# Splitting fp32 weights in a three-block decoder: part of the low halves on GpSimd instead of ScalarE plus an accumulating DMA

## The chip, the cores and the metric

The kernel runs on one core of one Trainium2 chip. The metric is device time in microseconds (us), the median over several runs. A second source of numbers is one profiled execution, from which the page, the groups of instructions, the windows, the waits and the timeline below are read.

## What is computed

A decoder with three kinds of blocks runs over one sequence of 256 tokens with 1024 features, all in fp32. Sixteen meta tokens are put ahead of it in block 1, so that block 1 works on 272. Cut to what matters here:

```
x = first_block(...)    # latent attention, then a gated linear recurrence (lru)
x = second_block(...)   # two hybrid layers, see below
x = third_block(...)    # retention, block attention, feed-forward

def hybrid_layer(x):                       # twice
    h = rms_norm(x, norm1_g);  proj = h @ w_in
    q, k, v, iq, ik, iw, a_in, c_in, g_in = split(proj)
    y_attn = sparse_attention(q, k, v, iq, ik, iw) @ w_attn_out
    a = causal_dwconv(a_val * sigmoid(a_gate), conf_conv_w) + b    # 31 taps
    y_conf = silu(layer_norm(a)) @ w_conf_out
    y_sc = (c_b * causal_dwconv(c_c * c_x, sc_conv_w)) @ w_sc_out  # 3 taps
    x = x + (g0 * y_conf + g1 * y_attn + g2 * y_sc) @ w_o          # g = sigmoid(g_in)
    return x + feed_forward(rms_norm(x, norm2_g))
```

## The kernel before

Weights come from HBM in **units** of 128 x 1024 fp32 (512 KB; some 128 x 848 or smaller). A product keeps fp32 accuracy with three fast matmuls: weight and activation are each split into a high part (rounded to the fast format) and a low part, the exact difference. `mm3` (L202 to L207) multiplies high by high, low weight by high activation, high weight by low activation, for each of the eight 128-row pieces of a unit: 24 matmuls of 256 or 272 columns a unit.

`emit_unit` (L166) makes a unit ready: a DMA issued by SyncE brings `raw`, ScalarE copies it to `whi` (L175), and `wlo` is made in one of two ways. Normally VectorE subtracts (L181). For a marked unit, ScalarE writes the negated copy into `wlo` (L178) and a DMA issued by GpSimd adds `raw` onto it (L179). `raw`, `whi` and `wlo` have five buffers each. `unit` (L189) hands out the next unit and sees to it that the three after it are emitted (`AHEAD = 3`). It also sets the marks: a running sum grows by `dma_share` with each unit, and a unit that brings it to 1 is marked.

The share is 0 outside the hybrid layers. In each hybrid layer it is 0.3 from the start (L900: token-major groups and the gated inputs `w_a2`), 0.625 from L1088 (the short convolution `w_c2`, with attention as side job, then `w_so`), 0.5 from L1119 (the gates `w_g2`, `w_g1` and the attention output `w_ao`), and 0 again from L1135.

Around the weights, VectorE carries most of the other work. The largest part of it in a hybrid layer are the 31-tap convolution's 240 multiply-adds (L924, `ca<-apad,vec,ca`), spread over these stages by a side job and held in their program order; they have to be through before the layer norm that follows the gates. GpSimd adds the finished convolution tiles to a sum (L931, `lnst`) and multiplies and adds the gated branches (L1125 and L1133, `mg`). In the recurrence, GpSimd multiplies `ii` by `rr` (L716) and adds squares (L326).

A scheduler orders the instructions of each engine ahead of time by dependences and its own costs; each engine then takes its list in that order.

Of the kernel before, what the change touches and what calls it, by code (L numbers as in the profile page):

```python
# [9 lines left out]
F32 = mybir.dt.float32  # L10
# [7 lines left out]
T1 = 272          # meta tokens + frames  # L18
T = 256
# [6 lines left out]
# Column offsets of the packed per-feature vectors (value of feature k*128+p at [p, off+k]).  # L26
# [29 lines left out]
class _Null:  # L56
    """Stands for every object of a pass that only lists the weight units in their order."""
# [17 lines left out]
class Prog:  # L75
    AHEAD = 3       # weight units split ahead of the one in use

    def __init__(self, tc, ins, out, dbg=None, plan=None):
        self.tc, self.nc, self.I, self.out = tc, tc.nc, ins, out
        self.dbg = dbg or {}  # L80
        self.plan = plan          # None: this pass lists the units
        self.specs, self.emitted, self.used = [], {}, 0
        self.jobs = []
        self.dma_share, self.share = 0.0, 0.0   # part of the units whose lo a DMA adds up
# [54 lines left out]
    @staticmethod  # L139
    def stagger(gens, depth):  # L140
        """Runs the generators in order, up to depth of them in flight, each a step behind."""
        gens, active = list(gens), []
        while gens or active:
            for g in list(active):
                try:
                    next(g)
                except StopIteration:
                    active.remove(g)
            if gens and len(active) < depth:
                g = gens.pop(0)  # L150
                next(g)
                active.append(g)
            yield

# [11 lines left out]
    def emit_unit(self, i):  # L166
        nc = self.nc
        name, m, c0, n, by_dma = self.plan[i]
# [3 lines left out]
        for a, b in ((0, n),) if i else ((0, n // 2), (n // 2, n)):  # L172
# [3 lines left out]
            if by_dma:  # L176
                # lo = -hi + raw, the sum made by an accumulating DMA: spares the vector engine
                nc.scalar.activation(lo[:, c], raw[:, c], AF.Copy, scale=-1.0)  # L178
                nc.gpsimd.dma_start(lo[:, c], raw[:, c], accum_op=ALU.add)  # L179
            else:  # L180
                nc.vector.tensor_sub(lo[:, c], raw[:, c], hi[:, c].bitcast(F32))  # L181
# [7 lines left out]
    def unit(self, name, m, c0, n):  # L189
        i = self.used  # L190
        self.used += 1
        self.share += self.dma_share
        by_dma = self.share >= 1.0
        self.share -= by_dma
        self.specs.append((name, m, c0, n, by_dma))
# [13 lines left out]
    def part(self, o, unit, xs, k0, k1, kt, base=0):  # L209
        """Contraction tiles k0..k1 of the output o; the unit starts at contraction tile base."""  # L210
# [7 lines left out]
    def tile_fm(self, name, m, kt, xs, t):  # L218
        """Feature-major output tile m: sum over kt contraction tiles; xs(k) -> (hi, lo)."""
# [6 lines left out]
    def lead_fm(self, name, ms, xs, t, ks, between=None):  # L226
        """Tiles ms of 8 contraction tiles, the first ks of all of them ahead of the others."""
# [9 lines left out]
    def tiles_of_unit(self, name, m, nt, kt, xs, t):  # L237
        """nt output tiles of few contraction tiles, packed in one unit."""
# [10 lines left out]
    def rsq(self, m, n, name):  # L249
        """1/sqrt of the positive columns m[:, :n]: bit seed, three Newton steps."""  # L250
# [10 lines left out]
    def cols(self, accs, segs, name):  # L261
        """Sums over features of each acc, per token, tokens on partitions (one column a segment)."""
# [29 lines left out]
    def rows(self, col, segs, name):  # L292
        """Column form [token, 1] -> the same values along the free dim, on every partition;
        a generator with one step between the vector engine's part and the rest."""
# [15 lines left out]
    def norm_rows(self, accs, segs, scales, eps, name):  # L310
        """1/rms of each token, for each acc, as rows. A generator; the first step is empty."""
# [51 lines left out]
    def consts(self):  # L363
# [17 lines left out]
        # the tensor engine runs while it waits for the first data, and so comes to its full clock  # L381
# [4 lines left out]
    def late(self, ins):  # L386
        """Keeps an instruction behind those of its engine that come before it here."""
        self.tc.keep_in_program_order(ins)

    def after(self, ins, first):  # L390
        """Keeps an instruction behind an earlier one of its engine."""
# [4 lines left out]
    def more_consts(self):  # L396
# [10 lines left out]
        self.caus = cp.tile([128, 2, T], F32, name="caus")      # 1 where the key is later  # L407
# [5 lines left out]
    def decay_rate(self):  # L413
        """softplus(-lam) = max(-lam, 0) + log1p(exp(-|lam|)); log1p(e) = 2 atanh(e / (2 + e))"""
# [22 lines left out]
    def mla(self):  # L437
# [13 lines left out]
        # latents: tiles kv 0..1, q 2..4  # L451
# [9 lines left out]
        # shared rope key, twice down the partitions  # L461
# [27 lines left out]
        def gate_tile(i):  # L489
            o = self.tile_fm("w_a_in", 6 + i, 8, xs, T1)  # L490
            dve.tensor_mul(gate[:, i], o, rb)
            # 2 silu(x) = x (1 + tanh(x / 2)); the half follows with the product
# [9 lines left out]
        # keys and values  # L502
# [18 lines left out]
        # queries: units of two tiles  # L521
# [64 lines left out]
        def meta():  # L586
            """The meta queries of all heads, over the meta keys."""
# [59 lines left out]
    def residual(self, name, kt, xs, x, t, t0, gains, g2=None, lead=(2, 6), between=None):  # L647
        """x += w^T xs, tile by tile; then the scaled split of x and the sums of its squares
        for the norm that follows. gains: key of the gain columns (or an AP of columns)."""
# [18 lines left out]
    def lru(self):  # L668
# [8 lines left out]
        last = [None]  # L677

        def gates(g):
            """The decay and what it leaves to the input, from the gates of two feature tiles."""  # L680
# [6 lines left out]
        def block(g):  # L687
# [5 lines left out]
            if g % 2:  # L693
                gates(g - 1)
                gates(g)
                # sqrt(1 - a^2) = (1 + a) sqrt((1 - a) / (1 + a))
# [37 lines left out]
        # from here on, the frames only: nothing that follows looks at the meta tokens  # L734
# [25 lines left out]
    def final_norm(self):  # L760
        """The final norm of block 1 and the first norm of block 2 in one: columns of both."""
# [13 lines left out]
    def final_x(self):  # L775
        """The output of block 1, the residual stream of the blocks that follow."""
# [12 lines left out]
    def norm_full(self, src, g, name):  # L789
        """The normalised stream, split: src(k) * g(k) * row factor."""  # L790
# [10 lines left out]
    def proj_tok(self, name, g, n, dst):  # L801
        """Group g of a token-major projection of the un-normalised split."""
# [14 lines left out]
    def rope_tok(self, v3, nh, half, cs):  # L817
        """In place on v3 [128, nh, 2*half]; cs [128, 4*half] = cos|cos|-sin|sin."""
# [10 lines left out]
    def attend(self, pairs, nk, mask, scales, pv):  # L829
        """Softmax attention of nh heads over nk keys for one tile of 128 queries, in steps.  # L830
        pairs: (queries^T, keys^T) per head; mask [128, nk] is added; scales: a positive column
        per head; pv(pt): takes the transposed probabilities, [keys, nk/128, nh * 128]."""
# [37 lines left out]
    def hybrid(self, layer):  # L870
# [7 lines left out]
        # ---- token-major columns, first group; the normalised stream meanwhile  # L878
# [21 lines left out]
        self.dma_share = 0.3  # L900
# [8 lines left out]
        # ---- gated depthwise convolution branch: inputs; its taps are spread over what follows  # L909
# [23 lines left out]
        # ---- attention, as side jobs. Columns: index queries 512, index key 64, weights 8,  # L933
        # values 256, keys 256, queries 1024
        qT = self.big("qT", 8, T)
        kiT = self.big("kiT", 7, T)      # 0-1 keys, 2-5 index queries, 6 index key twice
# [6 lines left out]
        # gain of the query dims that are not rotated, 1 for those that are  # L943
# [58 lines left out]
        def index(j, b, hds):  # L1002
            """Index scores of the heads hds (of one parity) added up for query tile j."""
# [84 lines left out]
        self.dma_share = 0.625  # L1088
# [3 lines left out]
        # ---- short gated convolution branch  # L1092
# [17 lines left out]
        # ---- gates and outputs of the branches  # L1110
# [8 lines left out]
        self.dma_share = 0.5  # L1119
# [15 lines left out]
        self.dma_share = 0.0  # L1135
# [53 lines left out]
        # ---- feed-forward with a short convolution  # L1189
# [24 lines left out]
    def ffn(self, name, g, finish):  # L1214
        """22 pairs of feature tiles of the normed stream; finish(first, second, i) takes each.
        The first pairs use the un-normalised split, while the normalised one is made."""
# [30 lines left out]
    def third(self):  # L1247
# [4 lines left out]
        rot = rm[:, 0:512]               # cos|cos|-sin|sin, 64 each, for each token tile  # L1252
# [6 lines left out]
        # columns: rq 512, rk 512, mq 512, mk 512 | mv 512 | rv 1024  # L1259
# [60 lines left out]
        # block attention: one block of 256 keys, so plain causal attention within it  # L1320
# [3 lines left out]
        def moba(j, q4, par):  # L1324
            """Heads 4*q4 + par and 4*q4 + par + 2, whose rows start at 64 * par."""
# [21 lines left out]
        # retention: scores with keys on partitions, outputs token-major, then transposed  # L1347
# [70 lines left out]
        # retention gate, then gates, outputs, mixture  # L1418
# [56 lines left out]
def _fm(w):  # L1475
    """[K, N] -> [N/128, 128, K] tiles: [m, p, k*128+c] = w[k*128+p, m*128+c]."""
# [5 lines left out]
def _tm(w, n):  # L1482
    """[K, groups*n] -> [groups * K/256, 128, 2n]: units of two contraction tiles."""
# [7 lines left out]
def _cols(v):  # L1491
    """[..., n*128] -> [128, ... * n]"""
    return np.asarray(v).reshape(-1, 128).T
# [41 lines left out]
def pack(inp):  # L1535
# [14 lines left out]
    # block 1  # L1550
# [24 lines left out]
    # block 2  # L1575
# [25 lines left out]
    # block 3  # L1601
# [26 lines left out]
```

## Time and profile before

| what | value |
|---|---|
| median of 3 runs | 1784.89 us (1782.8 to 1785.49) |
| span of the profiled execution | 1786.7 us |
| TensorE (PE) busy | 1752.1 us, 98% |
| VectorE (DVE) busy | 1359.8 us, 76% |
| ScalarE (ACT) busy | 1104.8 us, 62% |
| GpSimd (POOL) busy | 197.5 us, 11% |
| granted TensorE clock, mean | 0.995 of full speed |
| marked units (L178, L179) | 85 |

The page has no device time of the profiled execution other than its span, from the first to the last instruction; the 1786.7 us lie 1.8 us above the median of the runs. Busy shares are means over the whole span; stages differ, and a window of the trace shows one stage. Idle time is given with what ended it. Times of a group are sums of its instructions; in a window, busy time counts overlapping instructions of one engine once.

### The profile page before, as it was taken

To read this page: it belongs to the slowest core of one execution; us is meant where nothing else is said; L and a number is where in the kernel's file an instruction comes from. 1 tells how busy PE (TensorE), PEld (TensorE's weight loads), DVE (VectorE), ACT (ScalarE), POOL (GpSimd) and SP (SyncE) were. 2 spreads that over 40 slices of the span, in tenths; PEclk is the share of its full clock that TensorE was granted. 3 is DMA by queue.
4 is the path that set the end of the run, shared out by engine and by line. 5 is a ranking of instruction groups with operands and counts; after the bars stand their busy time and mean duration, and the time that the engine had idled before them with its cause. 6 is when DMAs were issued, how large, how long until landed. Compare 5 with 4: busy or idle time off the path is not lost.

```text
span 1786.7 us, 34523 instructions
## 1 busy us (share of the span) xinstructions
PE 1752.1 (98%) x13450; PEld 1694.4 (95%) x13450; DVE 1359.8 (76%) x2769; ACT 1104.8 (62%) x1870; POOL 197.5 (11%) x231
## 2 busy tenths in 40 slices
PE   8999899999999999999999999999999999999999
PEld 8879889999999999999998999999998889999999
DVE  7658898876998898756876898899857667786553
ACT  5646957678657576546578755766644666455442
POOL 3001130121230100011011131000000000010000
PEclk9999999999999999999999999999999999999999
DMA  7314367799995656667799997556565534655563
GB/s 261 124 60 140 121 188 223 206 258 240 251 251 178 207 170 191 178 181 217 199 255 242 243 254 232 183 165 201 173 200 191 173 96 154 196 176 187 179 181 103
DMA packets 97492, 340.68 MB, mean 191 GB/s; under 512 B 11024, under 2 KB 12064, under 8 KB 97328
## 3 DMA queue, kind: packets, MB, share of 16 engines
q1 hardware_dynamic: 84384, 292.51, 51.3%
q0 software_dynamic: 12944, 45.97, 13.4%
q8 instruction: 105, 1.72, 0.4%
q14 instruction: 59, 0.48, 0.1%
HBM read 293.90 MB, written 1.05 MB: 165 GB/s over the span
## 4 chain that ended last, share of the span: by engine, by line
PE 81%; DMA 8%; DVE 4%; ACT 4%; issue 3%; POOL 1%; SPq 0%; POOLq 0%; DVEq 0%; ACTq 0%
PE acc L205 22%; PE acc L206 22%; PE acc L207 22%; DMA wlo<-raw 5%; PE tok L205 3%; PE tok L206 3%; PE tok L207 3%; DMA raw<-w_c 2%; DVE ca L924 1%; ACT whi L175 1%; DVE wlo L181 1%; PE ix L1009 1%; PE lg L838 1%; PE po L1047 1%; ACT wlo L178 1%
## 5 line engine op out<-in xcount | busy, mean ns | idle before, releaser
L175 ACT ACTIVATE whi<-raw 128x1024 fp32r<-128x1024 f32 (+3 forms) x573 | 584.8, 1025 | 345.8 <-PE acc L207 163.3
L181 DVE TENSOR_TENSOR wlo<-raw,whi 128x1024 fp32r<-128x1024 f32 (+3 forms) x488 | 581.7, 1194 | 223.2 <-ACT whi L175 215.0
L206 PE MATMUL acc<-bh,wlo 128*128 128x256 f32 x1984 | 562.5, 284 | 14.7 <-DMA wlo<-raw 14.7
L205 PE MATMUL acc<-bh,whi 128*128 128x256 f32 x1984 | 566.2, 286 | 0.0
L207 PE MATMUL acc<-bl,whi 128*128 128x256 f32 x1984 | 560.7, 283 | 0.0
L206 PEld LDWEIGHTS acc<-bh,wlo 128*128 128x128 f32 x1984 | 380.7, 192 | 17.7 <-DMA wlo<-raw 17.3
L205 PEld LDWEIGHTS acc<-bh,whi 128*128 128x128 f32 x1984 | 380.8, 192 | 3.7 <-ACT wlo L178 1.0
L207 PEld LDWEIGHTS acc<-bl,whi 128*128 128x128 f32 x1984 | 380.3, 192 | 0.1
L924 DVE SCALAR_TENSOR_TENSOR ca<-apad,vec,ca 128x226 f32<-128x226 f32 (+14 forms) x480 | 243.5, 509 | 10.4 <-ACT ca L920 1.0
L206 PE MATMUL acc<-ah,wlo 128*128 128x256 f32 (+1 forms) x528 | 153.9, 291 | 5.9 <-DVE wlo L181 5.8
L205 PE MATMUL acc<-ah,whi 128*128 128x256 f32 (+1 forms) x528 | 155.5, 295 | 1.0 <-ACT whi L175 0.7
L207 PE MATMUL acc<-al,whi 128*128 128x256 f32 (+1 forms) x528 | 153.1, 290 | 0.0
L205 PE MATMUL acc<-fh,whi 128*128 128x256 f32 x528 | 149.4, 283 | 0.0
L206 PE MATMUL acc<-fh,wlo 128*128 128x256 f32 x528 | 149.4, 283 | 0.0
L207 PE MATMUL acc<-fl,whi 128*128 128x256 f32 x528 | 149.4, 283 | 0.0
L326 POOL TENSOR_TENSOR st<-st,sq 128x256 f32<-128x256 f32 (+1 forms) x56 | 53.5, 970 | 720.6 <-ACT sq L324 720.5
L178 ACT ACTIVATE wlo<-raw 128x1024 fp32r<-128x1024 f32 (+1 forms) x85 | 87.8, 1034 | 58.1 <-PE acc L206 35.2
L179 POOL DMA_DIRECT2D wlo<-raw x85 | 74.3, 874 | 350.9 <-ACT wlo L178 125.2
L206 PEld LDWEIGHTS acc<-ah,wlo 128*128 128x128 f32 x528 | 103.3, 196 | 7.0 <-DVE wlo L181 6.9
L205 PEld LDWEIGHTS acc<-ah,whi 128*128 128x128 f32 x528 | 103.3, 196 | 2.6 <-ACT whi L175 1.0
L207 PEld LDWEIGHTS acc<-al,whi 128*128 128x128 f32 x528 | 103.2, 196 | 0.0
L205 PE MATMUL tok<-whi,ah 128*128 128x424 f32 (+1 forms) x272 | 101.7, 374 | 0.0
(543 smaller groups left out, 3469.9 us busy)
## 6 DMA issues: line engine op xcount, KB each, us to landing
raw<-w_up SPq DMA_DIRECT2D x88, 512.0 KB, 3.9
wlo<-raw POOLq DMA_DIRECT2D x73, 512.0 KB, 7.6
raw<-w_g SPq DMA_DIRECT2D x72, 512.0 KB, 5.3
raw<-w_c SPq DMA_DIRECT2D x48, 512.0 KB, 6.3
raw<-w_f SPq DMA_DIRECT2D x44, 512.0 KB, 3.6
raw<-w_t SPq DMA_DIRECT2D x40, 424.0 KB, 3.4
raw<-w_a SPq DMA_DIRECT2D x32, 512.0 KB, 5.1
raw<-w_dn SPq DMA_DIRECT2D x32, 512.0 KB, 3.6
```

The costliest lines, as they stand in the source:

```text
L175: nc.scalar.activation(hi[:, c], raw[:, c], AF.Copy)
L178: nc.scalar.activation(lo[:, c], raw[:, c], AF.Copy, scale=-1.0)
L179: nc.gpsimd.dma_start(lo[:, c], raw[:, c], accum_op=ALU.add)
L181: nc.vector.tensor_sub(lo[:, c], raw[:, c], hi[:, c].bitcast(F32))
L205: mm(out, wh, xh, start=start, stop=False)
L206: mm(out, wl, xh, start=False, stop=False)
L207: mm(out, wh, xl, start=False, stop=stop)
L326: nc.gpsimd.tensor_add(acc[:, :n], acc[:, :n], q[:, :n])
L838: te.matmul(ps[:, i * nk:(i + 1) * nk], q, k, start=True, stop=True)
L924: tap = dve.scalar_tensor_tensor(ca[:, i, d:], ga[:, i, :T - d], w(j), ca[:, i, d:], op0=ALU.mult, op1=ALU.add)
L1009: te.matmul(ps[:, i * nk:(i + 1) * nk], kiT[o:o + 64, 2 + hd // 2, q], kiT[o:o + 64, 6, :nk], start=True, stop=True)
L1047: te.matmul(po, tok[k][:, 584 + g * 128:584 + (g + 1) * 128], ptb[:, k * n:(k + 1) * n], start=k == 0, stop=k == j)
```

## The change

The negated ScalarE copy and the accumulating DMA go. A marked unit's low part is now subtracted by GpSimd, the same operation that VectorE does for an unmarked one. The shares in the hybrid layers stay as they were. There is one more: 0.4 from the start of `lru`, the recurrence of block 1, where no unit was marked before. Comments were taken out, which shifts the line numbers by up to four.

```
-            if by_dma:
-                # lo = -hi + raw, the sum made by an accumulating DMA: spares the vector engine
-                nc.scalar.activation(lo[:, c], raw[:, c], AF.Copy, scale=-1.0)
-                nc.gpsimd.dma_start(lo[:, c], raw[:, c], accum_op=ALU.add)
-            else:
-                nc.vector.tensor_sub(lo[:, c], raw[:, c], hi[:, c].bitcast(F32))
+            eng = nc.gpsimd if by_pool else nc.vector
+            eng.tensor_sub(lo[:, c], raw[:, c], hi[:, c].bitcast(F32))
...
-        self.share += self.dma_share
-        by_dma = self.share >= 1.0
-        self.share -= by_dma
+        self.share += self.pool_share
+        by_pool = self.share >= 1.0
+        self.share -= by_pool
...
     def lru(self):
...
+        self.pool_share = 0.4
...
-        self.dma_share = 0.3
+        self.pool_share = 0.3
...
-        self.dma_share = 0.625
+        self.pool_share = 0.625
...
-        self.dma_share = 0.5
+        self.pool_share = 0.5
...
-        self.dma_share = 0.0
+        self.pool_share = 0.0
```

The order of instructions on GpSimd in the gates stage of the first hybrid layer (`mg` is the branch sum, `lnst` the convolution's sum, `wlo` a low part), before:

```order
L1133 TENSOR_TENSOR mg<-mg,sg 128x256
L179 DMA wlo<-raw 128x1024
L1133 TENSOR_TENSOR mg<-mg,sg 128x256
L179 DMA wlo<-raw 128x1024
L931 TENSOR_TENSOR lnst<-lnst,ca 128x256
```

and with the change:

```order
L1130 TENSOR_TENSOR mg<-mg,sg 128x256
L177 TENSOR_TENSOR wlo<-raw,whi 128x1024
L1130 TENSOR_TENSOR mg<-mg,sg 128x256
L177 TENSOR_TENSOR wlo<-raw,whi 128x1024
L928 TENSOR_TENSOR lnst<-lnst,ca 128x256
```

Each DMA issue has become a subtraction of 1024 columns in the same place of GpSimd's list, 96 of them in all with the 11 of the recurrence.

The order on GpSimd in the recurrence of block 1 (`st` sums squares, `ii` and `rr` belong to the recurrence), before:

```order
L326 TENSOR_TENSOR st_q<-st_q,sq 128x272 x2
L326 TENSOR_TENSOR st<-st,sq 128x272 x7
L716 TENSOR_TENSOR ii<-ii,rr 128x272 x8
L326 TENSOR_TENSOR st<-st,sq 128x256
L326 TENSOR_TENSOR st_2658<-st_2658,sq 128x256
```

and with the change:

```order
L322 TENSOR_TENSOR st<-st,sq 128x272
L177 TENSOR_TENSOR wlo<-raw,whi 128x1024 x3
L713 TENSOR_TENSOR ii<-ii,rr 128x272 x2
L177 TENSOR_TENSOR wlo<-raw,whi 128x1024
L713 TENSOR_TENSOR ii<-ii,rr 128x272 x2
L177 TENSOR_TENSOR wlo<-raw,whi 128x1024
```

Subtractions that stood in VectorE's list now stand between the multiplications of `ii` in GpSimd's, and start only after those ahead of them.

## Rows read from the trace of the kernel before

**Rows 1.** The page: busy time, share of the span and instructions of each engine.
```profile
PE 1752.1 (98%) x13450; PEld 1694.4 (95%) x13450; DVE 1359.8 (76%) x2769; ACT 1104.8 (62%) x1870; POOL 197.5 (11%) x231
```

**Rows 2.** Windows: length, busy us per engine (instructions), granted clock, DMA share, GB/s.
```profile
150.00:256.00 106.00, 98.81 (x757) 96.91 (x756) 95.23 (x176) 79.19 (x138) 23.46 (x25) 0.97 0.46 149
256.00:361.00 105.00, 102.06 (x684) 97.59 (x683) 89.67 (x237) 69.52 (x118) 15.47 (x21) 1.00 0.79 216
361.00:447.00 86.00, 83.56 (x658) 81.38 (x657) 62.61 (x187) 68.58 (x142) 14.36 (x17) 0.98 0.96 253
447.00:472.00 25.00, 25.00 (x202) 24.58 (x201) 23.99 (x47) 16.90 (x28) 4.81 (x6) 1.00 0.95 231
472.00:545.00 73.00, 70.32 (x586) 70.12 (x586) 69.09 (x112) 41.13 (x51) 26.04 (x30) 1.00 0.93 261
797.00:911.00 114.00, 112.54 (x762) 108.26 (x761) 87.06 (x213) 74.06 (x123) 15.33 (x21) 1.00 0.78 212
911.00:997.00 86.00, 81.53 (x653) 79.25 (x652) 64.68 (x191) 67.82 (x144) 14.72 (x17) 1.00 0.95 249
997.00:1023.00 26.00, 26.00 (x210) 25.58 (x209) 22.39 (x44) 18.10 (x31) 4.82 (x6) 1.00 0.90 225
1023.00:1096.00 73.00, 70.23 (x580) 69.58 (x579) 68.85 (x112) 40.98 (x51) 24.77 (x30) 1.00 0.93 260
```

**Rows 3.** Waits of TensorE: total us, times, longest.
```profile
PE acc L206 <- DMA wlo<-raw: 14.7, 12, 3.2
```

**Rows 4.** Windows of L178 alone, ScalarE's negated copies: busy us (count).
```profile
256.00:361.00 105.00, 12.03 (x12) 1.00 0.79 216
361.00:447.00 86.00, 15.68 (x15) 0.98 0.96 253
447.00:472.00 25.00, 5.29 (x5) 1.00 0.95 231
472.00:545.00 73.00, 9.55 (x9) 1.00 0.93 261
797.00:911.00 114.00, 12.78 (x13) 1.00 0.78 212
```

**Rows 5.** Groups by form, GpSimd: an uncontended 256-column and a 272-column two-input operation.
```profile
L1125 POOL TENSOR_TENSOR mg<-mg,sg 128x256 f32<-128x256 f32 x1 | 0.7, 732 | 1.5 <-ACT sg L1124 1.5
L326 POOL TENSOR_TENSOR st_kv<-st_kv,sq 128x272 f32<-128x272 f32 x1 | 0.8, 767 | 7.4 <-ACT sq L324 7.4
```

**Rows 6.** Groups, 504.2 to 505.0: GpSimd's L1133 and VectorE's two taps beside it.
```profile
L1133 POOL TENSOR_TENSOR mg<-mg,sg 128x256 f32<-128x256 f32 x1 | 0.9, 891 | 5.2 <-DVE sg L1132 5.2
L924 DVE SCALAR_TENSOR_TENSOR ca<-apad,vec,ca 128x236 f32<-128x236 f32 x1 | 0.8, 823 | 0.0
L924 DVE SCALAR_TENSOR_TENSOR ca<-apad,vec,ca 128x235 f32<-128x235 f32 x1 | 0.5, 455 | 0.0
```

**Rows 7.** Groups, 196.3 to 197.2: a 272-column GpSimd operation, VectorE before and beside it.
```profile
L716 POOL TENSOR_TENSOR ii<-ii,rr 128x272 f32<-128x272 f32 x1 | 0.8, 798 | 36.0 <-DVE rr L715 36.0
L713 DVE SCALAR_TENSOR_TENSOR rr<-aa,rr 128x272 f32<-128x272 f32 x1 | 0.4, 437 | 0.0
L713 DVE SCALAR_TENSOR_TENSOR rr<-aa,rr 128x272 f32<-128x272 f32 x1 | 1.0, 1012 | 0.0
```

**Rows 8.** Groups, 455.2 to 456.0: a tap beside an accumulating-DMA issue on GpSimd.
```profile
L924 DVE SCALAR_TENSOR_TENSOR ca<-apad,vec,ca 128x231 f32<-128x231 f32 x1 | 0.5, 460 | 0.0
L179 POOL DMA_DIRECT2D wlo<-raw x1 | 0.9, 885 | 1.7 <-ACT mg L1117 1.7
```

**Rows 9.** Timeline, 489.9 to 492.5: start us, us, engine, line; a DMA issue, two additions, a tap.
```profile
489.90 0.88 POOL L179 DMA_DIRECT2D wlo<-raw  x1 [3.41 <-ACT sg L1124]
490.50 1.74 POOL L1125 TENSOR_TENSOR mg<-mg,sg 128x256 f32<-128x256 f32 x2
490.36 2.17 DVE L924 SCALAR_TENSOR_TENSOR ca<-apad,vec,ca 128x249 f32<-128x249 f32 x1
```

**Rows 10.** Groups by form, VectorE: its own subtraction of a 1024-column unit.
```profile
L181 DVE TENSOR_TENSOR wlo<-raw,whi 128x1024 fp32r<-128x1024 f32 x420 | 515.2, 1229 | 187.6 <-ACT whi L175 179.4 <-PE tr L1282 4.8 <-PE acc L206 2.2
```

More of the change, by code (lines that the diff above doesn't have):

```diff
@@ L83, in __init__ @@
         self.jobs = []
-        self.dma_share, self.share = 0.0, 0.0
+        self.pool_share, self.share = 0.0, 0.0
     @classmethod
@@ L167, in emit_unit @@
         nc = self.nc
-        name, m, c0, n, by_dma = self.plan[i]
+        name, m, c0, n, by_pool = self.plan[i]
         raw = self.wp.tile([128, 1024], F32, name="raw", tag="raw", bufs=5)
@@ L191, in unit @@
         self.used += 1
-        self.share += self.dma_share
-        by_dma = self.share >= 1.0
-        self.share -= by_dma
-        self.specs.append((name, m, c0, n, by_dma))
+        self.share += self.pool_share
+        by_pool = self.share >= 1.0
+        self.share -= by_pool
+        self.specs.append((name, m, c0, n, by_pool))
         if self.plan is None:
```

## The prediction

> **What bounds the kernel now.** First the page's busy times [rows 1]: TensorE is busy for 98% of the span, VectorE for 76%, GpSimd for 11%. Taken alone that says that VectorE has a quarter of its time to spare and GpSimd nearly all of it. That share is a mean over stages with different limits, so the second view is the windows of the recurrence and of the two hybrid layers [rows 2], in which the change does all of its work. Read the third busy figure of each row, VectorE's, against the length. In order the rows are the recurrence (150 to 256), then for each hybrid layer the token groups with the gated inputs, the short convolution with attention, `w_so`, and the gates with `w_ao`. VectorE's idle time in them is 10.8 us (106.00 - 95.23), then 15.3, 23.4, 1.0 and 3.9 in the first layer and 26.9, 21.3, 3.6 and 4.2 in the second. So in `w_so` and the gates two engines are full at once: TensorE, and VectorE at 95%. Whatever takes VectorE's time there lengthens the stage. The third view is TensorE's waits [rows 3]: it waits 14.7 us in all, 12 times, for an accumulating DMA. That is the whole visible price of the path that the change removes.
>
> **What goes.** 85 negated copies leave ScalarE and 85 accumulating DMAs leave the queues. ScalarE has idle time in every window of [rows 2] (at the least 17.4 us of 86), so its relief is worth nothing by itself. The most that the removal can give is the 14.7 us of [rows 3]; I credit none of it in the sum, since these waits lie in windows which the next part makes longer for another engine, and keep it for a rival.
>
> **What comes: a subtraction of 1024 columns on GpSimd.** The trace has no such instruction; its nearest are GpSimd's two-input operations. An undisturbed one takes 732 ns for 256 columns and 767 ns for 272 [rows 5]: 35 ns for 16 columns, 2.19 ns a column. For 1024 columns that makes 0.73 + 768 x 0.00219 = 2.41 us, an estimate. On GpSimd itself this fits: in the gates nine of them add 21.7 us to the 26 us busy of a 73 us window, from which nine DMA issues of 0.88 us [rows 8] go.
>
> **What it does to VectorE is the step that decides.** In [rows 6] a GpSimd addition stands beside two taps of the 31-tap convolution. The first tap had begun before it and takes its usual 455 ns; the next takes 823 ns, 0.37 us more. In [rows 7] a 272-column GpSimd operation does the same to a VectorE operation that takes 437 ns just before: 1012 ns, 0.575 us more. So a VectorE operation that reads two operands from SBUF, as the taps and the subtractions of weights do, stands still while GpSimd reads two. Issuing a DMA on GpSimd does not have this effect: the tap beside one takes 460 ns [rows 8]. That is the difference between the two ways of making a low part. The old way costs VectorE nothing; the new one holds it up, though VectorE has no part in it.
>
> The price for 1024 columns has these bounds. Low: four times the tap's 0.37, 1.48 us. High: the whole duration, 2.41 us. Between them, [rows 7] in proportion to columns gives 0.575 x 1024 / 272 = 2.16 us, and [rows 6] plus 2.19 ns for each of 768 more columns gives 0.37 + 1.68 = 2.05 us. I take **2.05 us**, since the fixed part that a tap overlaps is paid once, however long the operation is.
>
> The Trainium skill's page SBUF — State Buffer, section Who interferes with whom, says that the shared port pair is held for the whole instruction and the other engine fully blocks. The tap row speaks against the whole instruction, with 0.37 us lost beside a 0.89 us operation; by the rule the price would be the high end, and the sum below 1880 us in place of 1848.
>
> **What is given back.** In nine places of the hybrid layers a GpSimd addition is queued right behind a DMA issue, and the tap beside it takes 1.5 to 2.2 us. One of them is [rows 9]: the tap lasts from 490.36 through the end of both additions, 2.17 us, 1.7 us more than a tap needs, of which two additions explain 0.74. With the DMA issue gone I give back 0.8 us for each, four in each gates stage (3.2 us) and one in the first `w_so`.
>
> **The sum.** The number of marked units a stage is the number of negated copies [rows 4]: 12, 15, 5 and 9 in the first layer, 13 and again 15, 5 and 9 in the second. A few of those in the token groups have 848 columns; I take all as 1024, at most 2 us a layer too many. I let the delay use up all of VectorE's idle time of the stage first, and count what is left as a longer stage:
> - first layer: 12 x 2.05 - 15.3 = 9.3; 15 x 2.05 - 23.4 = 7.4; 5 x 2.05 - 0.8 - 1.0 = 8.4; 9 x 2.05 - 3.2 - 3.9 = 11.3;
> - second layer: 13 x 2.05 is under 26.9, so 0; 30.8 - 21.3 = 9.5; 10.3 - 3.6 = 6.7; 18.5 - 3.2 - 4.2 = 11.1;
> - recurrence: 11 units now marked. They cost 11 x 2.05 = 22.6 us and spare VectorE 11 subtractions of 1.23 us [rows 10], 13.5 us. The 9.1 us left are under the 10.8 us idle, so 0.
>
> Together 63.7 us. Two things that I leave out have opposite signs: VectorE's operations on PSUM run on beside GpSimd, and its idle time cannot all be used, since some of it waits for TensorE. The profiled execution's 1786.7 us become 1850; it lies 1.8 us above the median of the runs, so the forecast is **1848 us**, 3.5% slower. With 1.48 us for the price the same sum is 25 us (1810), with 2.41 us it is 95.5 us (1880). That is the likeliest case's own range.
>
> **Rivals.**
> *The lead absorbs it; the DMA waits vanish.* Three units lie ready ahead of TensorE, some 9 us of its work (24 units take the 73 us of the gates), so a VectorE that is late by 2 us might never be noticed. Then the 14.7 us of [rows 3] are gained: 1770 us. It needs a small price: in the first layer's `w_so` and gates, 4.9 us idle and 4.0 us given back are shared by 14 subtractions, so the point is 0.64 us each. For it speaks that the tap rows show only 0.37 us; against it that those were for a quarter of the columns, and that a lead is used up once, while the delay comes with every second unit. Chance 0.07. Between 0.64 and about 1 us gain and loss cancel within 0.2% (3.6 us, about what a measurement of this kernel can tell from no change): 0.04. From there to 1.48 us the time is 1790 to 1810: 0.06.
>
> *VectorE's idle time is not to be had.* It sits where operations wait for ScalarE or TensorE, and GpSimd takes its list in order: a subtraction behind `lnst` waits until the taps of that tile are through, and one behind `ii` waits for VectorE's `rr`, as `ii` itself did for 36.0 us [rows 7]. TensorE would then wait for GpSimd, and VectorE for TensorE. With half of the idle time of the recurrence, the token groups and the short convolution usable, the five stages give 3.7, 16.9, 19.0, 13.2 and 20.1 us, with 37.5 from the others 110 us: 1895 us. With none at all it would be 1957. Chance 0.13.
>
> **How the numbers follow.** The forecast's case (1810 to 1880) has 0.70. The rival with unusable idle time adds its lower part, the mild cases theirs: 1800 to 1900 holds 8 in 10. Faster 0.07, the same 0.04, slower 0.89.
>
> **What would show it.** In the changed profile the GpSimd subtraction takes 2.3 to 3 us, with its wait for VectorE's running operation; taps beside it take about 2.5 us; TensorE's waits for DMA on `wlo` are gone and in their place stand waits for VectorE's and GpSimd's `wlo`, mostly in the gates; and those two stages are 10 to 12 us longer each. The prediction is wrong if taps beside a GpSimd subtraction stay under 1.1 us, or if they are stretched and the gates still take 73 us.

## The result, and the profile after

The changed kernel takes **1898.14 us** (median of 4 runs, 1895.29 to 1899.04) beside 1785.19 us for the kernel before on the same chip: a ratio of 1.0627, with a 95% interval of 1.0598 to 1.0657. The forecast was 1848 us in a range of 1800 to 1900. The time lies inside the range, 1.9 us under its end. The sign, the mechanism and the price of a subtraction were right; the sum came out at 63.7 us where 110.5 us were added to the span of the profiled execution.

The page of the changed kernel, its busy times (rows that answer to [rows 1]):

```profile
span 1897.2 us, 34298 instructions
...
PE 1788.5 (94%) x13450; PEld 1723.1 (91%) x13450; DVE 1513.9 (80%) x2758; ACT 1029.7 (54%) x1785; POOL 369.1 (19%) x242
```

VectorE has 154 us more busy time although 11 subtractions were taken from it. The same stages as in [rows 2], by the windows of the changed kernel (length; busy us of TensorE, its weight loads, VectorE, ScalarE, GpSimd, with counts; granted clock; DMA share; GB/s):

```profile
150.00:271.00 121.00, 106.72 (x771) 103.74 (x769) 100.54 (x167) 80.20 (x139) 52.76 (x36) 0.90 0.39 129
271.00:382.00 111.00, 105.46 (x691) 101.14 (x691) 103.62 (x228) 59.10 (x109) 37.73 (x22) 0.97 0.51 161
382.00:486.00 104.00, 87.74 (x657) 84.51 (x657) 96.58 (x196) 53.80 (x123) 40.00 (x19) 0.92 0.43 133
486.00:510.50 24.50, 23.21 (x186) 22.59 (x185) 23.90 (x31) 12.69 (x24) 12.53 (x6) 1.00 0.36 124
510.50:608.00 97.50, 77.70 (x597) 75.87 (x595) 94.70 (x127) 34.24 (x44) 43.08 (x30) 0.92 0.40 136
863.00:980.00 117.00, 112.50 (x763) 108.23 (x762) 101.47 (x205) 61.81 (x103) 34.19 (x20) 1.00 0.49 159
980.00:1085.00 105.00, 89.92 (x673) 86.69 (x671) 97.02 (x197) 55.77 (x136) 40.56 (x17) 0.92 0.39 131
1085.00:1108.00 23.00, 21.52 (x172) 20.85 (x171) 22.40 (x30) 12.08 (x23) 10.82 (x5) 1.00 0.33 115
1108.00:1205.30 97.30, 78.50 (x598) 75.28 (x597) 94.50 (x129) 34.03 (x45) 43.47 (x29) 0.95 0.41 139
```

The nine stages together went from 694 us to 800.3 us, 106 of the 110.5 us. In the gates (fifth and last row) VectorE is now busy for 97% and TensorE for 80%: the bound has moved from TensorE to VectorE. `w_so` did not become longer: its windows are a little shorter but hold fewer matmuls than those of [rows 2] (186 for 202, 172 for 210), and from the first to the last of its eight results that ScalarE copies out it takes 20.1 us in both kernels and both layers. The gates took 24.5 and 24.3 us more. VectorE makes 39 taps in the first `w_so` before and 24 after, and 89 and 104 in the gates behind it, so 15 taps that were through in `w_so` are now made in the gates. The two stages have to be read together.

What stretches VectorE is seen in one stretch of the first gates, by groups of the changed kernel, 551.4 to 553.8: GpSimd's subtraction and two taps in a row, the second of them beside it. Compare [rows 6].

```profile
L177 POOL TENSOR_TENSOR wlo<-raw,whi 128x1024 fp32r<-128x1024 f32 x1 | 2.6, 2557 | 0.0
L921 DVE SCALAR_TENSOR_TENSOR ca<-apad,vec,ca 128x229 f32<-128x229 f32 x1 | 2.5, 2486 | 0.0
L921 DVE SCALAR_TENSOR_TENSOR ca<-apad,vec,ca 128x228 f32<-128x228 f32 x1 | 0.8, 822 | 0.0
```

The tap beside the subtraction takes 2486 ns, 2.03 us more than the 455 ns of an undisturbed tap; the one before it, beside a 256-column addition, takes 822 ns as before. The price of 2.05 us for 1024 columns stands in the trace almost to the digit. TensorE's waits of the changed kernel (total us, times, longest) show what became of the wait for the DMA in [rows 3]:

```profile
PE acc L202 <- DVE wlo L177: 31.6, 22, 6.8
PE tr L989 <- DVE tok L824: 16.7, 3, 8.2
PE mups L1137 <- POOL lnst L928: 11.9, 2, 6.2
PE po L1044 <- ACT ptb L862: 8.3, 3, 4.5
PE acc L202 <- POOL wlo L177: 7.7, 7, 2.0
```

The DMA's 14.7 us are gone. TensorE now waits 31.6 us for VectorE's low parts (5.8 us before), 7.7 us for GpSimd's own, and 28.6 us at two places where there had been no wait worth a row: the transposes of the attention, behind VectorE's rotary embedding, and the layer norm's sum, behind the last tap.

### The profile page after: what moved, and what is told of

Read it like the earlier page. It is cut to its first block, busy times and chain, and to the rows that moved or that the text cites. A ratio compares the mean times of both kernels' runs of the same rounds, so it can differ in the third digit from the quotient of the medians.

```text
span 1897.2 us, 34298 instructions
## 1 busy us (share of the span) xinstructions
PE 1788.5 (94%) x13450; PEld 1723.1 (91%) x13450; DVE 1513.9 (80%) x2758; ACT 1029.7 (54%) x1785; POOL 369.1 (19%) x242
## 4 chain that ended last, share of the span: by engine, by line
PE 69%; DVE 22%; issue 4%; ACT 3%; POOL 1%; DMA 1%; SPq 0%; DVEq 0%; POOLq 0%; ACTq 0%
PE acc L201 19%; PE acc L203 19%; PE acc L202 18%; DVE ca L921 10%; DVE wlo L177 5%; PE tok L201 3%; PE tok L202 2%; PE tok L203 2%; ACT whi L175 1%; DVE cv L1101 1%; PE ix L1006 1%; PE lg L835 1%; PE s L537 0%; DVE zl L158 0%; DVE p L841 0%
## 5 line engine op out<-in xcount | busy, mean ns | idle before, releaser
L177 DVE TENSOR_TENSOR wlo<-raw,whi 128x1024 fp32r<-128x1024 f32 (+3 forms) x477 | 589.2, 1237 | 186.7 <-ACT whi L175 180.2
L202 PE MATMUL acc<-bh,wlo 128*128 128x256 f32 x1984 | 570.4, 288 | 32.1 <-DVE wlo L177 26.4
L201 PE MATMUL acc<-bh,whi 128*128 128x256 f32 x1984 | 574.2, 290 | 0.0
L203 PE MATMUL acc<-bl,whi 128*128 128x256 f32 x1984 | 567.8, 287 | 0.0
L202 PEld LDWEIGHTS acc<-bh,wlo 128*128 128x128 f32 x1984 | 388.5, 196 | 36.7 <-DVE wlo L177 29.4
L201 PEld LDWEIGHTS acc<-bh,whi 128*128 128x128 f32 x1984 | 389.0, 196 | 3.9 <-issue 1.3
L203 PEld LDWEIGHTS acc<-bl,whi 128*128 128x128 f32 x1984 | 387.8, 196 | 0.1
L921 DVE SCALAR_TENSOR_TENSOR ca<-apad,vec,ca 128x226 f32<-128x226 f32 (+14 forms) x480 | 329.9, 689 | 9.1
L177 POOL TENSOR_TENSOR wlo<-raw,whi 128x1024 fp32r<-128x1024 f32 (+1 forms) x96 | 244.1, 2547 | 281.6 <-ACT whi L175 257.8
L203 PE MATMUL tok<-wlo,ah 128*128 128x424 f32 (+1 forms) x272 | 101.3, 372 | 2.5 <-DVE wlo L177 2.5
```

The source lines that it names most:

```text
L177: eng.tensor_sub(lo[:, c], raw[:, c], hi[:, c].bitcast(F32))
L201: mm(out, wh, xh, start=start, stop=False)
L202: mm(out, wl, xh, start=False, stop=False)
L203: mm(out, wh, xl, start=False, stop=stop)
L921: tap = dve.scalar_tensor_tensor(ca[:, i, d:], ga[:, i, :T - d], w(j), ca[:, i, d:], op0=ALU.mult, op1=ALU.add)
```

## The experiments

Two theories were to be told apart. **The port**: VectorE stands still while GpSimd reads two operands, so each subtraction takes some 2 us of VectorE's time. **The lateness**: what hurts is that low parts come late out of GpSimd's list, or that the lead of three units is too short. A third question was why the sum was too small. The kernel before was timed again beside each group of runs, with medians from 1784.82 to 1789.97 us; each ratio is to the one beside it.

**Scratch subtraction on the kernel before.** The low parts stay with ScalarE and the DMA; GpSimd subtracts in addition, into a tile (`junk`) that nobody reads. Left-out lines of an edit are marked by dots.

```
                 nc.gpsimd.dma_start(lo[:, c], raw[:, c], accum_op=ALU.add)
+                for h in range(2):
+                    q = slice(a + h * (b - a) // 2, a + (h + 1) * (b - a) // 2)
+                    nc.gpsimd.tensor_sub(self.junk[:, :(b - a) // 2], raw[:, q], hi[:, q].bitcast(F32))
...
+        self.junk = cp.tile([128, 512], F32R, name="junk")
```

> The kernel before, with the low parts still made by ScalarE and the accumulating DMA; in addition, for each marked unit, GpSimd subtracts the same two operands into a scratch tile that nothing reads, in two halves of 512 columns. Theory (VectorE stands still while GpSimd reads two operands): the same lengthening as in the hybrid layers of the changed kernel, 70 to 100 us, so 1855 to 1885 us, with taps beside a half stretched by about 0.9 us each. Rival (the time is lost because the low parts come late out of GpSimd's list): nobody waits for the scratch, so 1783 to 1800 us.

Measured: 1902.27 us, a ratio of 1.0647 (1.0626 to 1.0669). This is 117 us over the kernel before on that chip, above the range expected, and as slow as the changed kernel, though nothing waits for the scratch. Groups of this run, 486.1 to 487.6, with one half and the two taps that it meets:

```profile
L182 POOL TENSOR_TENSOR junk<-raw,whi 128x512 fp32r<-128x512 f32 x1 | 1.3, 1341 | 0.1
L928 DVE SCALAR_TENSOR_TENSOR ca<-apad,vec,ca 128x229 f32<-128x229 f32 x1 | 1.4, 1396 | 0.0
L928 DVE SCALAR_TENSOR_TENSOR ca<-apad,vec,ca 128x230 f32<-128x230 f32 x1 | 1.4, 1390 | 0.0
```

Each half stretches a tap by 0.94 us, as expected. Why the whole was more than expected is not separated; two things that add to it are seen. One is GpSimd operations queued behind a DMA issue, the effect of [rows 9] at a larger size. The timeline of the same run (start us, us, engine, line):

```profile
514.30 0.87 POOL L179 DMA_DIRECT2D wlo<-raw  x1
514.91 1.04 POOL L1129 TENSOR_TENSOR mg<-mg,sg 128x256 f32<-128x256 f32 x1
515.60 1.58 POOL L182 TENSOR_TENSOR junk<-raw,whi 128x512 fp32r<-128x512 f32 x1
516.86 1.00 POOL L1129 TENSOR_TENSOR mg<-mg,sg 128x256 f32<-128x256 f32 x1
517.54 1.54 POOL L182 TENSOR_TENSOR junk<-raw,whi 128x512 fp32r<-128x512 f32 x1
...
514.64 4.93 DVE L928 SCALAR_TENSOR_TENSOR ca<-apad,vec,ca 128x231 f32<-128x231 f32 x1
```

One tap takes 4.93 us, through four GpSimd operations, and gets no turn between them. The other is in TensorE's waits of this run:

```profile
PE acc L209 <- DMA wlo<-raw: 42.7, 19, 4.2
```

These were 14.7 us in the kernel before. Nothing waits for the scratch itself, but the DMA issues stand behind it in GpSimd's list, so that low parts come later here too. Against the lateness this run proves less by itself than its expectation says; the next run keeps GpSimd as busy between the same issues.

**Scratch fills in place of scratch subtractions.** The same kernel, with GpSimd writing and reading nothing; the fills are held in program order.

```
                 nc.gpsimd.dma_start(lo[:, c], raw[:, c], accum_op=ALU.add)
+                for _ in range(5):
+                    self.late(nc.gpsimd.memset(self.junk, 0.0))
...
+        self.junk = cp.tile([128, 512], F32, name="junk")
```

> The kernel before, with the low parts still made by ScalarE and the accumulating DMA; in addition, for each marked unit, GpSimd fills a scratch tile of 512 columns five times, which reads nothing and keeps GpSimd about as busy as a subtraction. Theory (only GpSimd's reads hold VectorE up): taps beside a fill keep their 0.46 us, and the time is 1783 to 1800 us, the little above the kernel before being DMA issues that wait behind fills. Rival (any GpSimd operation holds VectorE up): 1855 to 1885 us.

Measured: 1786.15 us, a ratio of 1.0005 (0.9989 to 1.0021): no change clear of noise. By groups, GpSimd's fills of this run:

```profile
L181 POOL MEMSET junk<- 128x512 f32 x425 | 252.4, 594 | 18.4
```

These are 252 us of GpSimd's time, more than the 244.1 us of all subtractions of the changed kernel, and they cost nothing that the interval would show; TensorE's waits for the accumulating DMA are 11.2 us here. Groups of this run, 508.9 to 509.6, in the first gates: two fills, and the two taps beside them.

```profile
L181 POOL MEMSET junk<- 128x512 f32 x2 | 1.1, 525 | 0.1
...
L927 DVE SCALAR_TENSOR_TENSOR ca<-apad,vec,ca 128x239 f32<-128x239 f32 x1 | 0.5, 469 | 0.0
L927 DVE SCALAR_TENSOR_TENSOR ca<-apad,vec,ca 128x240 f32<-128x240 f32 x1 | 0.5, 469 | 0.0
```

Beside fills a tap keeps the time of an undisturbed one. VectorE's busy time on this run's page is 1364.4 us, 5 us above the kernel before; with scratch subtractions it is 1520.9 us. So it is GpSimd's reading of two operands, not its being busy or a DMA issue that waits behind it, that holds VectorE up (an operation that reads one was not run). The port theory stands. That lateness adds nothing is not shown by these two runs; the runs with a later need and a longer lead, below, bear on that. The Trainium skill's page SBUF — State Buffer, section Who interferes with whom, says that a VectorE instruction with two SBUF inputs contends with a GpSimd instruction that reads SBUF and not with one that only writes it; these two runs agree.

**Everything on VectorE.** On the changed kernel, all subtractions of marked units are VectorE's.

```
-            eng = nc.gpsimd if by_pool else nc.vector
+            eng = nc.vector
```

> The changed kernel with every subtraction on VectorE and none on GpSimd. Theory (what hurts is that a GpSimd subtraction of 1024 columns takes 2.1 us of VectorE's time, while VectorE itself needs 1.2 us): the 83 units of the hybrid layers cost VectorE about 100 us of work in place of 174, most of which fits into idle time outside w_so and the gates; by stage some 15 to 35 us over the kernel before, 1800 to 1820 us. Rival (any way without the DMA is as slow, since VectorE is full): within 20 us of the changed kernel, 1878 to 1900 us.

Measured: 1800.62 us, a ratio of 1.0078 (1.0057 to 1.0099), at the low end of the theory's range. VectorE doing 85 subtractions more costs 16 us; with GpSimd doing them, without the recurrence's share (the next run), it is 98.6 us, six times as much. TensorE's waits of this run:

```profile
PE mups L1137 <- POOL lnst L928: 21.0, 2, 10.5
```

By far the longest wait is one in each hybrid layer, for the layer norm behind the last tap. The kernel before has no such row; its 14.7 us of waits for the DMA are gone here. VectorE's busy time here is 77 us above the kernel before, and 61 us of that were absorbed.

**Without the recurrence's share.** On the changed kernel, no unit of the recurrence is marked.

```
-        self.pool_share = 0.4
```

> The changed kernel without the share of 0.4 in the recurrence of block 1, so that no unit is marked there and VectorE subtracts as before. Theory (each GpSimd subtraction costs VectorE about 2.1 us, and VectorE's idle time in the recurrence cannot be used): the recurrence and the start of the first hybrid layer come back by what they lost in the changed profile, some 18 to 21 us, so about 1878 us (1873 to 1884). Rival (the sum of the prediction: the 11 units fit into idle time there): no difference, 1895 to 1900 us.

Measured: 1883.4 us, a ratio of 1.0546 (1.0524 to 1.0567). The 11 units of the recurrence cost 15 us of the 113, less than theory's 18 to 21 and far from the rival's zero.

**The recurrence's share alone.** On the kernel before, GpSimd subtracts in the recurrence and nowhere else.

```
+        self.in_lru = False
...
-            if by_dma:
+            if by_dma == 2:
+                nc.gpsimd.tensor_sub(lo[:, c], raw[:, c], hi[:, c].bitcast(F32))
+            elif by_dma:
...
-        self.specs.append((name, m, c0, n, by_dma))
+        self.specs.append((name, m, c0, n, 2 * by_dma if self.in_lru else by_dma))
...
+        self.dma_share, self.in_lru = 0.4, True
...
-        self.dma_share = 0.3
+        self.dma_share, self.in_lru = 0.3, False
```

> The kernel before, with the accumulating DMA in the hybrid layers, and GpSimd subtractions in the recurrence alone, for the 11 units that the change marks there. Theory (the recurrence costs what the run without it gave back, 15 us, and the parts add up): 1797 to 1804 us; in its profile VectorE is held up there as in the changed kernel, and the sums of squares on GpSimd, which the norm behind the recurrence waits for, come later behind GpSimd subtractions. Rival (the prediction's sum, 9.1 us of added work for 10.8 us of idle time): 1783 to 1788 us.

Measured: 1796.28 us, a ratio of 1.0045 (1.0025 to 1.0065), some 8 us: slower, clear of the rival, and just under the range of the theory. It is about half of the 15 us, but by the intervals the two are 4 to 12 us here and 8 to 21 us there, so whether the parts add up is not shown. TensorE's waits in the recurrence are like those of the changed kernel: 3.5 us for VectorE's `ul` and 2.0 us for GpSimd's low part, where the kernel before has no such rows.

**Quarters.** Each GpSimd subtraction of the changed kernel is cut in four.

```
-            eng = nc.gpsimd if by_pool else nc.vector
...
+                for h in range(4):
+                    q = slice(a + h * (b - a) // 4, a + (h + 1) * (b - a) // 4)
+                    nc.gpsimd.tensor_sub(lo[:, q], raw[:, q], hi[:, q].bitcast(F32))
```

> The changed kernel with each GpSimd subtraction cut into four of 256 columns (212 for the smaller units). Theory (the price is GpSimd's reading time less a fixed overlap with VectorE's own operation, paid back once for each GpSimd instruction): a tap beside a quarter is stretched by about 0.37 to 0.5 us, 1.5 to 2.0 us for a unit in place of 2.1, and the time falls by some 10 to 50 us, 1850 to 1888 us. Rival (the lock goes to the next GpSimd instruction in its queue before VectorE gets a turn): the same total of stretching in fewer, longer taps, and no gain, 1893 to 1905 us.

Measured: 1856.27 us, a ratio of 1.0373 (1.0356 to 1.039), 42 us faster than the changed kernel with the same arithmetic. Groups of this run, 507.3 to 507.7, a tap beside a quarter:

```profile
L925 DVE SCALAR_TENSOR_TENSOR ca<-apad,vec,ca 128x234 f32<-128x234 f32 x1 | 0.8, 826 | 0.0
```

A tap beside a quarter loses 0.37 us, so a unit costs four times that, 1.48 us in place of 2.05: the low bound of the prediction, made real. GpSimd is busier (463.6 us in place of 369.1), VectorE less (1464.0 us in place of 1513.9), and the kernel faster. VectorE gets a turn between two quarters, and the overlap with its own running operation is had four times.

**A later need, and a longer lead.** On the changed kernel, in two runs: the matmuls that read the low part come after all those that read the high part; and four units are ready ahead.

```
-            self.mm3(o, wh[:, c], wl[:, c], xh, xl, k == 0, k == kt - 1)
...
+            mm(o, wh[:, c], xs(k)[0], start=k == 0, stop=False)
+            mm(o, wh[:, c], xs(k)[1], start=False, stop=False)
+        for k, c in zip(range(k0, k1), cs):
+            mm(o, wl[:, c], xs(k)[0], start=False, stop=k == kt - 1)
```
```
-    AHEAD = 3
+    AHEAD = 4
```

> The changed kernel with another order of the matmuls of a unit: the sixteen that read the high parts first, then the eight that read the low part, so that a low part is wanted some 2 us later. Theory (VectorE has too much work in the gates and the short convolution, so a later need only moves the wait): a gain of 0 to 15 us, 1883 to 1898 us. Rival (the low parts are only a little late, 33 waits for them of 1.3 us in the mean): most of the 41.8 us of these waits go, 1855 to 1870 us.

> The changed kernel with four units ready ahead in place of three. Theory (throughput of VectorE, and tiny operations of the attention chain that each wait out one GpSimd subtraction): a longer lead changes little, 1885 to 1900 us. Rival (bursts: VectorE's idle time could not be used since the lead was too short): 1860 to 1880 us.

Measured: 1898.55 us (ratio 1.0606, 1.0589 to 1.0623) and 1899.4 us (1.0615, 1.0596 to 1.0634). Neither shows a gain; one of 28 us or more, as the rival of the first has it, is far outside the intervals. In the first, the waits for low parts fall from 41.8 us to 26.3 and others take their place, by its list of TensorE's waits:

```profile
PE acc L214 <- DVE wlo L177: 23.8, 13, 5.2
PE tr L992 <- DVE tok L827: 21.9, 4, 6.4
PE mups L1140 <- POOL lnst L931: 15.7, 2, 9.0
```

A wait that is put off comes back elsewhere. That three units lie ready and not four is not why VectorE's idle time went unused, and a later need for low parts gives nothing back.

**High parts first on the kernel before.** The same reordering where TensorE is the bound and the waits are for a DMA.

> The kernel before, with the accumulating DMA, and the order of matmuls of the run above: high parts first, the low part of a unit wanted some 2 us later. Theory (TensorE's 14.7 us of waits for the accumulating DMA and 5.8 us for VectorE's low parts are each at most 3.2 us long, so a need that is 2 us later removes most of them): 8 to 18 us less, 1767 to 1777 us. Rival (TensorE is the bound and takes up the time elsewhere): 1781 to 1788 us.

Measured: 1780.13 us beside 1789.97 us, a ratio of 0.9949 (0.9932 to 0.9966), at the low end of the 8 to 18 us less. TensorE's waits of this run have 0.7 us for the DMA in place of 14.7:

```profile
PE acc L215 <- ACT whi L175: 3.8, 3, 2.4
...
PE acc L218 <- DMA wlo<-raw: 0.7, 2, 0.5
```

The waits are shorter by more than the kernel is. Since the gain is small, it was measured again:

> The same kernel as the run with the accumulating DMA and high parts first, in more rounds, since its gain is near what a measurement can tell. Theory: the gain holds, 0.3% to 0.8% under the kernel before on the same chip. Rival: it was the chip, and the difference is under 0.2%.

Measured: 1780.49 us beside 1788.24 us, a ratio of 0.9954 (0.9939 to 0.997). The gain holds: this version beats both kernels. The waits for the DMA are 5.2 us in the profile of this run, so the 0.7 us above are one execution's.

## Why the prediction came out as it did

**What bounds the kernel.** Right. `w_so` and the gates, where VectorE was at 95%, are where the largest part was lost: the first pair grew from 98 us to 122, the second from 99 to 120.3, 45 us of the 110, where the sum has 37.5.

**What goes.** Right as far as it can be seen. No stage shows a gain from the relief of ScalarE and of the DMA queues; by itself it was not measured. That the DMA's waits could be had without GpSimd is what the reordered kernel shows, at about half a per cent.

**What comes on GpSimd.** 2.41 us were estimated; the groups of the changed kernel have:

```profile
L177 POOL TENSOR_TENSOR wlo<-raw,whi 128x1024 fp32r<-128x1024 f32 x85 | 219.9, 2592 | 241.0 <-ACT whi L175 217.1 <-PE acc L202 14.2 <-DVE ca L921 9.4
```

One that began ahead of VectorE's operation takes 2.41 us, as the first line of the last timeline below (258.46) shows; the mean is 0.18 us longer.

**The price.** 2.05 us was taken, 2.03 us stand in the row above, and the runs with halves (0.94 us) and quarters (0.37 us) lie on the same line: 0.37 us for 256 columns and about 2.2 ns for each further one. By the rule in the Trainium skill's page SBUF — State Buffer, section SBUF: two separate sides, that whichever of the two instructions starts first has the shared ports for the whole instruction and the other engine fully blocks, it would be 2.56 us beside that subtraction; the trace has 0.5 us less.

**What is given back.** Right in kind: taps of 1.5 to 2.2 us beside additions are gone in the gates, where a tap beside an addition now takes 0.80 to 0.94 us.

**The sum failed in one term: how much of VectorE's idle time takes up the delay.** The sum's step "I let the delay use up all of VectorE's idle time of the stage first" is what did not hold. It let the delay use up the idle time of every stage first, 108 us over the nine stages. From the two sets of windows VectorE's idle time there fell from 110.4 us (694.0 - 583.6) to 65.6 us (800.3 - 734.7): 45 us were used. The added busy time was somewhat over-estimated in turn, 151 us in these windows where the terms sum to 172, as operations on PSUM run on beside GpSimd: three of them, `u<-acc,nb` at 173.06, take 0.43 us each inside a subtraction of 2.39 us. So 172 - 108 should have been 151 - 45. The largest misses are the short convolution (18 and 19 us for 7.4 and 9.5) and the recurrence (15 us for 0), whose idle time grew from 10.8 us to 20.5. The rival "VectorE's idle time is not to be had" with half of it usable gave 1895 us. Its total is near the measured one in part by luck, since its misses cancel: in the order of the rows, with `w_so` and the gates as one, it has 3.7, 16.9, 19.0, 19.7, 13.2, 20.1 and 17.8 us, and the windows have 15, 6, 18, 24, 3, 19 and 21.3. It fits the short convolution; the recurrence lost 11 us more and the token groups 10 us less. The first rival's limits do not follow from its own terms: with each stage's idle time and what is given back, loss and gain cancel at some 1.1 to 1.3 us a subtraction, not at 0.64 to 1; the measured 2.03 us lies above either.

The busy times of the runs say the same. VectorE's busy time over the kernel before, and the time over it: with VectorE's own subtractions 77 us and 16 us, with quarters 104 and 66, without the recurrence 150 and 98, the changed kernel 154 and 113, with scratch subtractions 161 and 117. Between 38 and 61 us are absorbed, never 108.

Why the idle time was not to be had is shown in part. In the recurrence a stretched VectorE operation makes TensorE wait, and VectorE's longest wait there is in turn for TensorE (1.5 us in the kernel before, 4.6 now). The changed kernel's timeline (first two lines), TensorE's waits from 150 to 275, and VectorE's from 150 to 271:

```profile
205.22 2.38 POOL L177 TENSOR_TENSOR wlo<-raw,whi 128x1024 fp32r<-128x1024 f32 x1 [0.95 <-ACT whi L175]
205.39 2.52 DVE L158 TENSOR_TENSOR ul<-uc,uh 128x272 fp32r<-128x272 f32 x1
PE acc L203 <- DVE ul L158: 3.4, 2, 2.5
DVE h L656 <- PE acc L203: 4.6, 2, 4.3
```

The `ul` operation ends at 207.91, 2.09 us later than undisturbed, and TensorE's wait of 2.5 us ends with it.

In the attention, VectorE's list has chains of tiny operations, one of which is seen in the timeline of the changed kernel, with a later stretch of the same list below it:

```profile
387.36 2.37 DVE L249 TENSOR_SCALAR rqks<-ms 128x10 int32<-128x10 int32 x1
389.77 2.32 DVE L250 TENSOR_SCALAR rqkz<-rqks 128x10 int32<-128x10 int32 x1
...
387.04 5.01 POOL L177 TENSOR_TENSOR wlo<-raw,whi 128x1024 fp32r<-128x1024 f32 x2
...
413.96 2.54 DVE L921 SCALAR_TENSOR_TENSOR ca<-apad,vec,ca 128x238 f32<-128x238 f32 x1
416.43 2.62 DVE L824 TENSOR_TENSOR tok<-tok,ropet 128x320 f32<-128x320 f32 x1
```

Two operations on ten columns take 2.3 us each beside two subtractions in a row; in the kernel before the same two take 0.16 and 0.17 us in the mean. The chain leads over the rotary embedding (L824) to TensorE's waits at the attention's transposes, 16.7 us. The longest of them in the first hybrid layer, 6.56 us, ends at 419.10 with the last line above: that addition and the tap before it, beside two more subtractions (412.96, 5.74 us), take 4.2 us more than undisturbed. That VectorE's idle time of the attention goes unused for the same reason is argued, not shown. At the end of the recurrence GpSimd itself is late: its sums of squares, which the next norm waits for, stand behind subtractions in its list, as this timeline of the changed kernel shows.

```profile
258.46 2.41 POOL L177 TENSOR_TENSOR wlo<-raw,whi 128x1024 fp32r<-128x1024 f32 x1
260.83 8.16 POOL L322 TENSOR_TENSOR st<-st,sq 128x256 f32<-128x256 f32 x8
268.96 2.80 POOL L177 TENSOR_TENSOR wlo<-raw,whi 128x848 fp32r<-128x848 f32 x1
271.73 3.74 POOL L322 TENSOR_TENSOR st<-st,sq 128x256 f32<-128x256 f32 x4
```

TensorE waited 3.7 us for the last of these sums. The recurrence's own units are not what that wait comes from: without them it is 3.2 us, behind a subtraction of the stage that follows.

A further part may be TensorE's clock: its granted mean is 0.90 in the recurrence and 0.92 in both short convolutions, from 0.97, 0.98 and 1.00 in [rows 2], which means stretches at the lower of its two levels, 1.2 GHz. One of them shows what came before: from 230 to 240 us TensorE is busy for 4.61 of 10 us, and the granted clock is 0.86 there and 0.63 in the next 10 us. By the two pages TensorE's busy time grew from 1752.1 to 1788.5 us for the same 13450 matmuls, so of the 110.5 us some 36 are longer matmuls and 74 are idle time. In the gates, with VectorE busy for 97%, a slower TensorE can cost little; in the other two its share of the loss was not separated from the rest, and no run was made that keeps the clock up. It stays open.

**The signs to look for.** The duration of the subtraction, the stretched tap, the vanished DMA wait and the new waits were all there. That `w_so` and the gates would be 10 to 12 us longer each was not: taps moved from the one to the other, and the pair counts.

## What to carry to other kernels

Before work is moved to GpSimd, look in the trace for a VectorE instruction beside a two-input GpSimd instruction and for one beside a fill: the difference is what the move costs VectorE, and in a stage where VectorE is full it can be more than VectorE's own time for the work (2.05 us for 1.23 us here). An engine's idle time in a window is not a reserve: here 45 of 110 us of it were used, and in the recurrence none. Count on it only where the trace shows what would run in it. If GpSimd has to read two operands beside a busy VectorE, try the instruction in pieces: quarters gave back 42 us here.

## What was not expected of the hardware

A GpSimd operation that is queued behind a DMA issue holds up even a tap that began before it (514.64 and 514.91 in the timeline above, where in [rows 6] such a tap kept its 455 ns), and operations queued one behind the other can do so together: one tap of 0.46 us took 4.93 us through four of them. Without a DMA issue in the queue, VectorE got one operation in between two subtractions, as at 387 and at 414 us in the changed kernel. Tiny operations lose as much as large ones: 2.2 us on 0.17. And more GpSimd time can be less VectorE time: quarters raised GpSimd's busy time by 94 us and took 42 us off the kernel.
